# Loading K, Q and V for two groups at a time, and storing the last two groups over the SP queue, in a linear-attention kernel

## The chip, the cores and the metric

The kernel runs on one core of a Trainium2 chip. The metric is the device time of one execution in microseconds. The engines are TensorE (PE in the profile; PEld is its weight load), VectorE (DVE), ScalarE (ACT), GpSimd (POOL) and SyncE (SP). A DMA is issued by an engine (here GpSimd or SP) and carried out by the core's 16 DMA engines.

## What is computed

Batch 8, heads 12, sequence 512, head dimension 64, all float32:

```
Q_feat = np.maximum(0, Q) + 1
K_feat = np.maximum(0, K) + 1
KV = np.einsum('bhkd,bhkv->bhdv', K_feat, V)
K_sum = np.sum(K_feat, axis=2)
numerator = np.einsum('bhqd,bhdv->bhqv', Q_feat, KV)
denominator = np.einsum('bhqd,bhd->bhq', Q_feat, K_sum)
out = numerator / (denominator[:, :, :, None] + 1e-10)
```

There are 96 pairs of batch and head. Q, K, V and the output have 12.58 MB each, so 50.3 MB cross the memory interface once.

## The kernel before, in words

The 96 pairs are worked off in NG = 12 groups of eight. A group's slice of K, of Q, of V and of the output is 1 MiB in float32 each. K, Q and V are cast to bf16 by the DMA that loads them (512 KB in SBUF for each), all but the K of group 0, which SP loads as float32.

**Tiles.** `k_raw` and `q_raw` hold one group's K or Q; their pool has IN_BUFS = 4 buffers each. V goes into one of NV = 3 tiles `v_blk`, each with five blocks: blocks 0 to 3 hold V in a block-diagonal pattern (each block is filled by one DMA on its own 32 partitions and is zero elsewhere), and block 4 holds a pattern of ones that makes the K sums come out of the same matmul. The zeros and ones are written once, at the start, by DVE memsets (L206, L212, L224), ACT copies (L207, L213, L225) and small DVE copies (L210, L216, L228). Group g uses `v_blk[g % 3]`. Results go into `o_sb`, of which there are OUT_BUFS = 6.

**Functions.** `load_k` (L86) and `load_q` (L100) issue one DMA each, `load_v` (L93) four. `store` issues one DMA on GpSimd (L107), or, for the last group, two halves on SP (L110). `k_features` and `q_features` make max(x + 1, 1) on DVE, two instructions each (L116). `keys_values` does 32 matmuls (L141) into `kva_ps` and copies it into `kva_diag` on ACT (L151, L152). `transposes` turns the Q features on TensorE (L160) and copies them on ACT (L161). `output` does 32 matmuls (L173) into `o_ps` in four parts; DVE takes the reciprocal (L183) and multiplies (L184) part by part.

**Order.** The order on every engine is the order of the program text (`manual_schedule`); waits are put in by the framework where data or buffers need them. The loop at L231 does, for group g: features of g, transposes of g-1, output of g-2, keys_values of g, then the loads of group g+3 (AHEAD = 3) and the store of group g-3 (LAG = 3). So on GpSimd's queue the order is K, V, Q of group g+3 and then the store of g-3, and a waiting DMA holds up all that stand behind it. Before the loop the loads of groups 0, 1 and 2 are issued, between the memsets. After the loop the last group is finished and the stores of groups 8 to 11 are issued.

A tile may be written again when its readers are done: V of group g+3 waits for keys_values(g), K of group g+3 for k_features(g-1), Q of group g+3 for q_features(g-1).

Of the kernel before, what the change touches and what calls it, by code (L numbers as in the profile page):

```python
# [8 lines left out]
FP32 = mybir.dt.float32  # L9
BF16 = mybir.dt.bfloat16  # L10
ALU = mybir.AluOpType

BANK = 512
IN_BUFS = 4
OUT_BUFS = 6
LAG = 3
AHEAD = 3


@with_exitstack  # L20
def kernel(
# [4 lines left out]
    V: bass.AP,  # L26
    out: bass.AP,
):

# [5 lines left out]
    nc = tc.nc  # L37

    B, H, S, D = Q.shape
    P = 128  # L40
    C = 8
    C2 = 2 * C
    NPAIR = B * H * S // (P * C)
    NP = 4
    NG = NPAIR // NP
# [3 lines left out]
    def view(t, c):  # L49
        return t.flatten_outer_dims().rearrange("(n p c) d -> p n c d", p=P, c=c)  # L50

    q_dram = view(Q, C2)
    k_dram = view(K, C2)
    v_dram = view(V, C2)
    o_dram = view(out, C)

    const = ctx.enter_context(tc.tile_pool(name="const", bufs=1))
    head_pool = ctx.enter_context(tc.tile_pool(name="head_pool", bufs=1))
    in_pool = ctx.enter_context(tc.tile_pool(name="in_pool", bufs=IN_BUFS))
    feat_pool = ctx.enter_context(tc.tile_pool(name="feat", bufs=2))  # L60
# [6 lines left out]

    identity = const.tile([P, P], BF16, name="identity")
    NV = 3
    v_blk = [const.tile([P, 5, 2, C2, D], BF16, name=f"v_blk{i}") for i in range(NV)]  # L70
    ones = const.tile([P, 4], BF16, name="ones")
    zero = const.tile([P, 1], FP32, name="zero")
    kva_diag = [const.tile([P, 4, 2, D1], BF16, name=f"kva_diag{i}") for i in range(NV)]

    k_in = {}
    q_in = {}
    kfs = {}
# [1 line left out]
    qts = {}  # L79
    outs = {}  # L80

    def load_k(g):
        k_raw = (head_pool if g == 0 else in_pool).tile(
            [P, 2, C2, D], FP32 if g == 0 else BF16, name="k_raw"
        )
        (nc.sync if g == 0 else nc.gpsimd).dma_start(  # L86
            out=k_raw, in_=k_dram[:, g * 2 : g * 2 + 2]
        )
        k_in[g] = k_raw

    def load_v(g):
        for b in range(4):
            nc.gpsimd.dma_start(  # L93
                out=v_blk[g % NV][32 * b : 32 * b + 32, b],
                in_=v_dram[32 * b : 32 * b + 32, 2 * g : 2 * g + 2],
            )

    def load_q(g):
        q_raw = in_pool.tile([P, 2, C2, D], BF16, name="q_raw")
        nc.gpsimd.dma_start(out=q_raw, in_=q_dram[:, g * 2 : g * 2 + 2])  # L100
        q_in[g] = q_raw

    def store(g):
        o_sb = outs.pop(g)
        o_to = o_dram[:, g * NP : g * NP + NP]
        if g < NG - 1:
            nc.gpsimd.dma_start(out=o_to, in_=o_sb)  # L107
            return
        for h in range(2):
            nc.sync.dma_start(out=o_to[:, h:NP:2], in_=o_sb[:, h:NP:2])  # L110

    def edge(i):
        return v_blk[i][:, 4, :, :, 0:4].rearrange("p n c j -> p (n c) j")

    def feature(dst, src):
        nc.vector.tensor_scalar(  # L116
# [3 lines left out]
    def k_features(g):  # L120
        k_raw = k_in.pop(g)
        kf = feat_pool.tile([P, C2, 2, D], BF16, name="kf")
        for n in range(2):
            feature(kf[:, :, n], k_raw[:, n])
        kfs[g] = kf

    def q_features(g):
        q_raw = q_in.pop(g)
        qf = feat_pool.tile([P, C2, 2, D], BF16, name="qf")
        for half in range(2):  # L130
            cs = slice(half * C, half * C + C)
            feature(qf[:, cs].rearrange("p c n d -> p n c d"), q_raw[:, :, cs])
        qfs[g] = qf

    def keys_values(g):
        kf = kfs.pop(g)
        vb = v_blk[g % NV]
        kva_ps = psum_kva.tile([P, 5, D], FP32, name="kva_ps")
        for c in range(C2):
            for n in range(2):  # L140
                nc.tensor.matmul(  # L141
                    kva_ps[64 * n : 64 * n + 64],
                    lhsT=kf[:, c, n, :],
                    rhs=vb[:, :, n, c, :],
                    start=(c == 0),
                    stop=(c == C2 - 1),
                )
        kva = kva_diag[g % NV]
        for n in range(2):
            ps = slice(64 * n, 64 * n + 64)  # L150
            nc.scalar.copy(out=kva[ps, :, n, 0:D], in_=kva_ps[ps, 0:4, :])  # L151
            nc.scalar.copy(out=kva[ps, :, n, D], in_=kva_ps[ps, 4, 0:4])  # L152

    def transposes(g):
        qf = qfs.pop(g)
        qt = mid_pool.tile([P, C, P, 2], BF16, name="qt")
        for half in range(2):
            qt_ps = psum_qt.tile([P, C, P], BF16, name="qt_ps")
            for c in range(C):
                nc.tensor.transpose(qt_ps[:, c, :], qf[:, half * C + c, :, :], identity)  # L160
            nc.scalar.copy(out=qt[:, :, :, half], in_=qt_ps)  # L161
        qts[g] = qt

    def output(g):
# [26 lines left out]
                )  # L191
        outs[g] = o_sb

    with tc.manual_schedule():
        nc.gpsimd.memset(zero, 0.0)  # L195
        load_k(0)
        load_q(0)
        load_k(1)
        load_q(1)
        nc.vector.memset(ones, 0.0)  # L200
        for b in range(4):
            nc.vector.memset(ones[32 * b : 32 * b + 32, b : b + 1], 1.0)  # L202
        flat = [t.rearrange("p b n c d -> p (b n c d)").bitcast(FP32) for t in v_blk]
        width = flat[0].shape[1]
        part = width * 4 // 7
        nc.vector.memset(flat[0][:, 0:part], 0.0)  # L206
        nc.scalar.copy(  # L207
            out=flat[0][:, part:width], in_=zero.to_broadcast([P, width - part])
        )
        nc.vector.tensor_copy(out=edge(0), in_=ones[:, None, :].to_broadcast([P, 2 * C2, 4]))  # L210
        load_v(0)
        nc.vector.memset(flat[1][:, 0:part], 0.0)  # L212
        nc.scalar.copy(  # L213
            out=flat[1][:, part:width], in_=zero.to_broadcast([P, width - part])
        )
        nc.vector.tensor_copy(out=edge(1), in_=ones[:, None, :].to_broadcast([P, 2 * C2, 4]))  # L216
        make_identity(nc, identity)
        for t in kva_diag:
            nc.gpsimd.memset(t, 0.0)  # L219
        load_v(1)  # L220
        load_k(2)
        k_features(0)
        q_features(0)
        nc.vector.memset(flat[2][:, 0:part], 0.0)  # L224
        nc.scalar.copy(  # L225
            out=flat[2][:, part:width], in_=zero.to_broadcast([P, width - part])
        )
        nc.vector.tensor_copy(out=edge(2), in_=ones[:, None, :].to_broadcast([P, 2 * C2, 4]))  # L228
        load_v(2)
        load_q(2)  # L230
        for g in range(NG - 1):  # L231
            if g:
                k_features(g)
                q_features(g)
                transposes(g - 1)
            if g >= 2:
                output(g - 2)
            keys_values(g)
            if g + AHEAD < NG:
                load_k(g + AHEAD)  # L240
                load_v(g + AHEAD)
                load_q(g + AHEAD)
            if g >= LAG:
                store(g - LAG)
        last = NG - 1
        k_features(last)
        transposes(last - 1)
        output(last - 2)
        q_features(last)
        keys_values(last)  # L250
        transposes(last)
        output(last - 1)
        output(last)
        for g in range(last - LAG, NG):
            store(g)
# [30 lines left out]
```

## Time and profile before

| | us |
|---|---|
| median of 13 runs | 129.56 |
| lowest, highest | 129.02, 130.9 |
| the profiled execution's own time | 129.52 |
| its span, first to last instruction | 127.8 |

Busy shares of the span: TensorE 58%, weight load 42%, DVE 52%, ACT 37%, GpSimd 42%. The DMA traffic, by the profile's own count, is 37.75 MB read and 12.58 MB written, 394 GB/s over the span. The profile's row of GB/s counts the bytes that arrive, so a load that casts float32 to bf16 counts half of what it reads, and a store counts in full.

The page has the busy time of each engine, the span in 40 slices, the DMA queues, the chain of work that ended last, the costliest groups of instructions, and the DMA issues. Beside it the trace answers by time: the instructions of one engine in order, and busy time and DMA traffic in any stretch.

### The profile page before, as it was taken

How to read it: one execution, taken by the hardware profiler on the slowest of the kernel's cores; microseconds unless marked ns; L12 is line 12 of the kernel's file. 1: busy time of each engine (PE TensorE's matmuls, PEld its weight loads, DVE VectorE, ACT ScalarE, POOL GpSimd, SP SyncE). 2: the span in 40 equal slices, each digit the busy share in tenths (PEclk: the TensorE clock that was granted, in tenths of full speed). 3: DMA queues.
4: the chain of work that ended last, by engine and by line, in shares of the span. 5: the costliest groups of instructions: out<-in, count | busy, mean ns of one | idle time of the engine just before them, and what ended most of it. 6: DMA issues, size and time to landing. Idle time of an engine off the chain costs nothing.

```text
span 127.8 us, 2373 instructions
## 1 busy us (share of the span) xinstructions
PE 73.9 (58%) x960; PEld 54.0 (42%) x960; DVE 66.3 (52%) x155; ACT 47.2 (37%) x76; POOL 54.2 (42%) x92
## 2 busy tenths in 40 slices
PE   0000099839968297855804982991992896956000
PEld 0000077626656275644603651771661664834000
DVE  4898702085292955929309407615624825679300
ACT  7940006940546408291540063036027019180000
POOL 6695775516346274544442272282264240202000
PEclk9999999975699959999996577568559559996555
DMA  3999999999999999999999999999999999999970
GB/s 91 327 212 210 207 209 207 210 210 207 212 207 214 207 208 212 208 342 239 207 312 272 202 276 309 208 249 337 207 232 345 216 213 383 419 412 419 403 296 0
DMA packets 13914, 32.13 MB, mean 251 GB/s; under 512 B 1360, under 2 KB 1360, under 8 KB 13904
## 3 DMA queue, kind: packets, MB, share of 16 engines
q0 software_dynamic: 13088, 29.89, 99.4%
q1 hardware_dynamic: 816, 2.10, 4.6%
q8 instruction: 7, 0.11, 0.3%
q14 instruction: 3, 0.02, 0.0%
HBM read 37.75 MB, written 12.58 MB: 394 GB/s over the span
## 4 chain that ended last, share of the span: by engine, by line
DMA 63%; DVE 8%; PE 8%; POOL 8%; issue 6%; POOLq 0%
DMA k_raw<-in_K_dram 28%; DMA q_raw<-in_Q_dram 25%; DMA out_dram<-o_sb 10%; DVE o_sb L184 6%; POOL v_blk L93 6%; PE kva_ps L141 5%; PE qt_ps L160 2%; POOL q_raw L100 1%; PE o_ps L173 1%; DVE recip L183 1%; POOL k_raw L86 1%; DVE qf L116 1%; POOL zero L195 0%; POOLq L107 0%; POOLq L93 0%
## 5 line engine op out<-in xcount | busy, mean ns | idle before, releaser
L141 PE MATMUL kva_ps<-v_blk,kf 128*64 128x320 bf16 x384 | 42.3, 396 | 15.8 <-DMA v_blk<-in_V_dram 15.8
L141 PEld LDWEIGHTS <-kf 128*64 128x64 bf16 x384 | 28.8, 147 | 25.0 <-DVE qf L116 15.7
L93 POOL DMA_DIRECT2D v_blk<-in_V_dram x48 | 26.4, 554 | 28.0 <-DMA k_raw<-in_K_dram 12.1
L173 PE MATMUL o_ps<-kva_diag,qt 128*64 128x130 bf16 x384 | 21.1, 251 | 28.6 <-DVE o_sb L184 28.1
L184 DVE TENSOR_TENSOR o_sb<-o_ps,recip 128x512 f32<-128x512 f32 x48 | 33.2, 692 | 1.7
L151 ACT CAST kva_diag<-kva_ps 64x256 bf16<-64x256 f32 x24 | 8.9, 371 | 66.4 <-PE kva_ps L141 66.1
L161 ACT COPY qt<-qt_ps 128x1024 bf16<-128x1024 bf16 x24 | 29.6, 1301 | 0.3
L173 PEld LDWEIGHTS <-qt 128*64 128x64 bf16 x384 | 14.0, 123 | 34.6 <-DVE o_sb L184 32.8
L116 DVE TENSOR_SCALAR qf<-q_raw 128x1024 bf16<-128x1024 bf16 x24 | 9.2, 427 | 32.5 <-DMA q_raw<-in_Q_dram 32.5
L107 POOL DMA_DIRECT2D out_dram<-o_sb x11 | 8.5, 771 | 21.3 <-DMA q_raw<-in_Q_dram 7.0
L116 DVE TENSOR_SCALAR kf<-k_raw 128x1024 bf16<-128x1024 bf16 (+1 forms) x24 | 10.9, 498 | 11.1 <-DMA k_raw<-in_K_dram 5.6
L160 PE MATMUL qt_ps<-identity,qf 128*128 128x128 bf16 x192 | 14.0, 231 | 0.0
L160 PEld LDWEIGHTS <-qf 128*128 128x128 bf16 x192 | 11.9, 105 | 4.4 <-issue 4.2
L183 DVE RECIPROCAL recip<-o_ps 128x8 f32<-128x8 f32 x48 | 9.6, 199 | 4.9 <-PE o_ps L173 4.9
L86 POOL DMA_DIRECT2D k_raw<-in_K_dram x11 | 7.8, 713 | 8.7 <-DMA out_dram<-o_sb 5.5
L100 POOL DMA_DIRECT2D q_raw<-in_Q_dram x12 | 8.8, 730 | 4.2 <-DMA v_blk<-in_V_dram 2.5
L152 ACT CAST kva_diag<-kva_ps 64x4 bf16<-64x4 f32 x24 | 4.1, 169 | 0.0
L206 DVE MEMSET v_blk<- 128x2925 f32 x1 | 2.5, 2496 | 0.7 <-DVE ones L202 0.7
L224 DVE MEMSET v_blk<- 128x2925 f32 x1 | 2.5, 2496 | 0.6 <-issue 0.6
L212 DVE MEMSET v_blk<- 128x2925 f32 x1 | 2.5, 2496 | 0.6 <-issue 0.6
L219 POOL MEMSET kva_diag<- 128x520 bf16 x3 | 2.0, 718 | 0.0
L207 ACT COPY v_blk<-zero 128x2195 f32<-128x2195 f32 x1 | 2.0, 2019 | 0.0
(15 smaller groups left out, 7.9 us busy)
## 6 DMA issues: line engine op xcount, KB each, us to landing
out_dram<-o_sb POOLq DMA_DIRECT2D x11, 1024.0 KB, 11.9
q_raw<-in_Q_dram POOLq DMA_DIRECT2D x12, 512.0 KB, 10.8
v_blk<-in_V_dram POOLq DMA_DIRECT2D x48, 128.0 KB, 9.4
k_raw<-in_K_dram POOLq DMA_DIRECT2D x11, 512.0 KB, 12.0
k_raw<-in_K_dram SPq DMA_DIRECT2D x1, 1024.0 KB, 4.8
out_dram<-o_sb SPq DMA_DIRECT2D x2, 512.0 KB, 5.9
```

The lines of the kernel that those rows point to most:

```text
L86: (nc.sync if g == 0 else nc.gpsimd).dma_start(out=k_raw, in_=k_dram[:, g * 2 : g * 2 + 2])
L93: nc.gpsimd.dma_start(out=v_blk[g % NV][32 * b : 32 * b + 32, b], in_=v_dram[32 * b : 32 * b + 32, 2 * g : 2 * g + 2],)
L100: nc.gpsimd.dma_start(out=q_raw, in_=q_dram[:, g * 2 : g * 2 + 2])
L107: nc.gpsimd.dma_start(out=o_to, in_=o_sb)
L116: nc.vector.tensor_scalar(out=dst, in0=src, scalar1=1.0, scalar2=1.0, op0=ALU.add, op1=ALU.max)
L141: nc.tensor.matmul(kva_ps[64 * n : 64 * n + 64], lhsT=kf[:, c, n, :], rhs=vb[:, :, n, c, :], start=(c == 0), stop=(c == C2 - 1),)
L151: nc.scalar.copy(out=kva[ps, :, n, 0:D], in_=kva_ps[ps, 0:4, :])
L160: nc.tensor.transpose(qt_ps[:, c, :], qf[:, half * C + c, :, :], identity)
L161: nc.scalar.copy(out=qt[:, :, :, half], in_=qt_ps)
L173: nc.tensor.matmul(ops[c // 4][64 * j : 64 * j + 64, c // 2 % 2, (c % 2) * W : (c % 2) * W + W], lhsT=qt[:, c, 32 * b : 32 * b + 32, :], r ...
L183: nc.vector.reciprocal(out=recip, in_=cells[:, :, :, :, D:D1])
L184: nc.vector.tensor_tensor(out=o_sb[:, h:NP:2, 4 * i : 4 * i + 4].rearrange("p n (b c) d -> p b c n d", b=2), in0=cells[:, :, :, :, 0:D], i ...
```

## The change

K and Q are loaded for two groups with one DMA, and V for two groups with four DMAs, for groups 2 and 3, 4 and 5, 6 and 7, 8 and 9. Groups 0, 1, 10 and 11 are loaded one by one as before. The K and Q tiles are twice as large and there are two of each (IN_BUFS = 2), so the space is the same. The three V tiles become one tile `v_all` of nine blocks for two double buffers: blocks 0 to 3 are buffer 0, blocks 5 to 8 buffer 1, and block 4 (the ones) is shared; a matmul reads blocks 0 to 4 or blocks 4 to 8. Each block holds two groups, and a group's half is `own(g)`.

The loads in the loop are issued after keys_values of the odd groups 1, 3, 5 and 7, for the pair that starts three groups on, in the order K, V, Q; for groups 10 and 11, after group 7, as K, V, Q of 10 and then K, V, Q of 11. The store of g-3 stays at its place in the loop, behind them. The stores of groups 10 and 11, and not of 11 alone, go over SP in halves. The zeroing at the start is cut differently: three blocks by DVE and two by ACT for group 0 and for group 1, then two blocks each by DVE and ACT for the pair of groups 2 and 3.

```diff
-IN_BUFS = 4
+IN_BUFS = 2
 OUT_BUFS = 6
 LAG = 3
-AHEAD = 3
...
-    v_blk = [const.tile([P, 5, 2, C2, D], BF16, name=f"v_blk{i}") for i in range(NV)]
+    v_all = const.tile([P, 9, 4, C2, D], BF16, name="v_all")
+    v_blk = [v_all[:, 5 * i : 5 * i + 4] for i in range(2)]
...
+    def own(g):
+        return slice(g % 2 * 2, g % 2 * 2 + 2)
+
+    def load_k(s, groups):
+        if groups == (0,):
+            k_raw = head_pool.tile([P, 2, C2, D], FP32, name="k_first")
+            nc.sync.dma_start(out=k_raw, in_=k_dram[:, 0:2])
+            k_in[0] = k_raw
+            return
+        if s not in k_bufs:
+            k_bufs[s] = in_pool.tile([P, 4, C2, D], BF16, name="k_raw")
+        ms = slice(groups[0] % 2 * 2, groups[-1] % 2 * 2 + 2)
+        nc.gpsimd.dma_start(
+            out=k_bufs[s][:, ms], in_=k_dram[:, 2 * groups[0] : 2 * groups[-1] + 2]
+        )
+        for g in groups:
+            k_in[g] = k_bufs[s][:, own(g)]
+
+    def load_v(s, groups):
+        ms = slice(groups[0] % 2 * 2, groups[-1] % 2 * 2 + 2)
         for b in range(4):
             nc.gpsimd.dma_start(
-                out=v_blk[g % NV][32 * b : 32 * b + 32, b],
-                in_=v_dram[32 * b : 32 * b + 32, 2 * g : 2 * g + 2],
+                out=v_blk[s % 2][32 * b : 32 * b + 32, b, ms],
+                in_=v_dram[32 * b : 32 * b + 32, 2 * groups[0] : 2 * groups[-1] + 2],
             )
...
+    def load(s):
+        pair = (2 * s, 2 * s + 1)
+        for groups in ((pair,) if s < NG // 2 - 1 else ((pair[0],), (pair[1],))):
+            load_k(s, groups)
+            load_v(s, groups)
+            load_q(s, groups)
 
     def store(g):
         o_sb = outs.pop(g)
         o_to = o_dram[:, g * NP : g * NP + NP]
-        if g < NG - 1:
+        if g < NG - 2:
             nc.gpsimd.dma_start(out=o_to, in_=o_sb)
             return
...
     def keys_values(g):
         kf = kfs.pop(g)
-        vb = v_blk[g % NV]
+        sb = g // 2 % 2
+        vb = v_all[:, 4 * sb : 4 * sb + 5, own(g)]
...
-            nc.scalar.copy(out=kva[ps, :, n, 0:D], in_=kva_ps[ps, 0:4, :])
-            nc.scalar.copy(out=kva[ps, :, n, D], in_=kva_ps[ps, 4, 0:4])
+            nc.scalar.copy(out=kva[ps, :, n, 0:D], in_=kva_ps[ps, sb : sb + 4, :])
+            nc.scalar.copy(out=kva[ps, :, n, D], in_=kva_ps[ps, 4 - 4 * sb, 0:4])
...
+        clear((0, 5), own(0), 3)
+        mark(own(0))
+        load_v(0, (0,))
+        clear((0, 5), own(1), 3)
+        mark(own(1))
         make_identity(nc, identity)
         for t in kva_diag:
             nc.gpsimd.memset(t, 0.0)
-        load_v(1)
-        load_k(2)
+        load_v(0, (1,))
+        load_k(1, (2, 3))
         k_features(0)
         q_features(0)
...
+        clear((5, 9), slice(0, 4), 7)
+        load_v(1, (2, 3))
+        load_q(1, (2, 3))
         for g in range(NG - 1):
...
             keys_values(g)
-            if g + AHEAD < NG:
-                load_k(g + AHEAD)
-                load_v(g + AHEAD)
-                load_q(g + AHEAD)
+            if g % 2 and g // 2 + 2 < NG // 2:
+                load(g // 2 + 2)
             if g >= LAG:
                 store(g - LAG)
```

`clear(blocks, ms, parts)` zeroes blocks up to `parts` on DVE and the rest on ACT; `mark(ms)` writes the ones of block 4 on DVE; `load_q` is changed as `load_k` is.

More of the change, by code (lines that the diff above doesn't have):

```diff
@@ L73 @@
     kva_diag = [const.tile([P, 4, 2, D1], BF16, name=f"kva_diag{i}") for i in range(NV)]
+    k_bufs = {}
+    q_bufs = {}
     k_in = {}
@@ L80, with load_q @@
     outs = {}
-    def load_k(g):
-        k_raw = (head_pool if g == 0 else in_pool).tile(
-            [P, 2, C2, D], FP32 if g == 0 else BF16, name="k_raw"
-        )
[L86 to L91, printed above, removed]
+    def own(g):
[11 more added lines that the diff above has]
+            out=k_bufs[s][:, ms], in_=k_dram[:, 2 * groups[0] : 2 * groups[-1] + 2]
+        )
+        for g in groups:
+            k_in[g] = k_bufs[s][:, own(g)]
+    def load_v(s, groups):
+        ms = slice(groups[0] % 2 * 2, groups[-1] % 2 * 2 + 2)
         for b in range(4):
             nc.gpsimd.dma_start(
-                out=v_blk[g % NV][32 * b : 32 * b + 32, b],
-                in_=v_dram[32 * b : 32 * b + 32, 2 * g : 2 * g + 2],
-            )
[L98 to L101, printed above, removed]
+                out=v_blk[s % 2][32 * b : 32 * b + 32, b, ms],
+                in_=v_dram[32 * b : 32 * b + 32, 2 * groups[0] : 2 * groups[-1] + 2],
+            )
+    def load_q(s, groups):
+        if s not in q_bufs:
+            q_bufs[s] = in_pool.tile([P, 4, C2, D], BF16, name="q_raw")
+        ms = slice(groups[0] % 2 * 2, groups[-1] % 2 * 2 + 2)
+        nc.gpsimd.dma_start(
+            out=q_bufs[s][:, ms], in_=q_dram[:, 2 * groups[0] : 2 * groups[-1] + 2]
+        )
+        for g in groups:
+            q_in[g] = q_bufs[s][:, own(g)]
+    def load(s):
[4 more added lines that the diff above has]
+            load_q(s, groups)
     def store(g):
@@ L110, in store @@
             nc.sync.dma_start(out=o_to[:, h:NP:2], in_=o_sb[:, h:NP:2])
-    def edge(i):
-        return v_blk[i][:, 4, :, :, 0:4].rearrange("p n c j -> p (n c) j")
     def feature(dst, src):
@@ L192, in output, with clear, mark @@
         outs[g] = o_sb
+    def clear(blocks, ms, parts):
+        for eng, bs in zip((nc.vector, nc.scalar), (slice(blocks[0], parts), slice(parts, blocks[1]))):
+            t = v_all[:, bs, ms].rearrange("p b m c d -> p b (m c d)").bitcast(FP32)
+            if eng is nc.vector:
+                eng.memset(t, 0.0)
+            else:
+                eng.copy(out=t, in_=zero[:, :, None].to_broadcast([P, t.shape[1], t.shape[2]]))
+    def mark(ms):
+        e = v_all[:, 4, ms, :, 0:4].rearrange("p m c j -> p (m c) j")
+        nc.vector.tensor_copy(out=e, in_=ones[:, None, :].to_broadcast([P, e.shape[1], 4]))
     with tc.manual_schedule():
         nc.gpsimd.memset(zero, 0.0)
[L196 to L199, printed above, removed]
+        for g in range(2):
+            load_k(0, (g,))
+            load_q(0, (g,))
         nc.vector.memset(ones, 0.0)
@@ L202 @@
             nc.vector.memset(ones[32 * b : 32 * b + 32, b : b + 1], 1.0)
[L203 to L216, printed above, removed]
+        clear((0, 5), own(0), 3)
[3 more added lines that the diff above has]
+        mark(own(1))
         make_identity(nc, identity)
@@ L219 @@
             nc.gpsimd.memset(t, 0.0)
-        load_v(1)
-        load_k(2)
+        load_v(0, (1,))
+        load_k(1, (2, 3))
         k_features(0)
         q_features(0)
[L224 to L230, printed above, removed]
+        clear((5, 9), slice(0, 4), 7)
+        load_v(1, (2, 3))
+        load_q(1, (2, 3))
         for g in range(NG - 1):
```

## The prediction, made before the changed kernel ran

> **What bounds the kernel now.** I read the 40 slices first, then busy time and traffic by stretch, then DVE and GpSimd in order of time. The slices say that the DMA engines never rest:
>
> ```profile
> DMA  3999999999999999999999999999999999999970
> GB/s 91 327 212 210 207 209 207 210 210 207 212 207 214 207 208 212 208 342 239 207 312 272 202 276 309 208 249 337 207 232 345 216 213 383 419 412 419 403 296 0
> ```
>
> The rate row counts arriving bytes: 210 is 420 GB/s read by a casting load, as fast as the 419 of the stores at the end. By stretch (last two columns: DMA share, GB/s):
>
> ```profile
> 26.00:54.00 28.00, 20.87 (x286) 15.54 (x288) 18.39 (x48) 11.04 (x19) 13.32 (x22) 0.82 1.12 210
> ...
> 107.00:118.00 11.00, 7.48 (x128) 5.55 (x128) 8.97 (x23) 4.80 (x8) 1.50 (x2) 0.90 1.03 418
> 118.00:123.00 5.00, 0.29 (x6) 0.04 (x2) 1.24 (x3) 0.00 (x0) 0.00 (x0) 0.50 1.02 402
> ```
>
> Compute engines wait for loads; the DVE timeline shows Q of groups 3 to 10 landing, each releasing DVE (start, duration, ..., idle before):
>
> ```profile
> 34.23 0.76 DVE L116 TENSOR_SCALAR qf<-q_raw 128x1024 bf16<-128x1024 bf16 x2 [3.63 <-DMA q_raw<-in_Q_dram]
> 41.71 0.76 DVE L116 TENSOR_SCALAR qf<-q_raw 128x1024 bf16<-128x1024 bf16 x2 [2.66 <-DMA q_raw<-in_Q_dram]
> 49.26 0.76 DVE L116 TENSOR_SCALAR qf<-q_raw 128x1024 bf16<-128x1024 bf16 x2 [2.76 <-DMA q_raw<-in_Q_dram]
> 56.76 0.76 DVE L116 TENSOR_SCALAR qf<-q_raw 128x1024 bf16<-128x1024 bf16 x2 [2.70 <-DMA q_raw<-in_Q_dram]
> ...
> 97.56 0.76 DVE L116 TENSOR_SCALAR qf<-q_raw 128x1024 bf16<-128x1024 bf16 x2 [4.17 <-DMA q_raw<-in_Q_dram]
> ```
>
> From 34.23 to 56.76 three groups of loads pass, 22.53/3 = 7.51 us each, 2.5 per MiB. So the n-th MiB in queue order lands at about 4.2 + 2.5n: Q3, the 12th, at 34.2; Q4, the 15th, at 41.7. From 56.76 to 97.56 each group also has a store: 40.80/4 = 10.20, so a store there costs 2.69, against 1.049 MB / 418 GB/s = 2.51 among stores: 0.18 more. All 48 MiB with 5 such stores give 4.2 + 120 + 0.9 = 125.1. The last store, issued on SP at 119.30, takes 5.9 us: 125.2. The other 2.6 us of the 127.8 are the close of the program, and 1.72 lie around the span. So the time is the sum of DMA work, and compute matters only where it leaves the queue empty.
>
> GpSimd waits, too. V's first DMA of group 5 waits, as do the other three:
>
> ```profile
> 42.26 0.54 POOL L93 DMA_DIRECT2D v_blk<-in_V_dram  x1 [1.64 <-DMA q_raw<-in_Q_dram]
> 44.51 1.76 POOL L93 DMA_DIRECT2D v_blk<-in_V_dram  x3 [1.71 <-DMA k_raw<-in_K_dram]
> ```
>
> By the chain of waits the K that landed at 44.23 was issued at 32.29, eight GpSimd DMAs earlier. The same count holds at 29.47 (K issued at 17.93) and 70.13 (store issued at 57.31): at most eight are under way, some 4 to 5 MiB.
>
> **What the skill says.** "DMA: Bandwidth & Descriptors", section "Issuing engines are not separate DMA queues": queues of all engines share 16 DMA engines, so moving a store to SP saves issue time only. The trace agrees: SP's stores end at 402 GB/s, not above 418. Same page, "Anatomy of one DMA": a fixed cost of about 2 us per DMA, mostly completion latency. Here it hides behind queued work: K of group 5 landed 2.5 us after Q4 (44.23 - 41.71), and V (four DMAs) with Q took 49.26 - 44.23 = 5.03, again 2.5 each. "HBM Reference", "Specifications": a core alone streams about 425 GB/s; 418 to 420 here is near it.
>
> **The change, part by part.**
>
> *Fewer DMAs.* Before: 82 on GpSimd, 3 on SP. After: K 7, Q 8, V 2x4 + 4x4 + 2x4 = 32, stores 10 on GpSimd; 5 on SP. 85 become 62, 23 fewer. V's three extra DMAs cost at most 5.03 - 2x2.5, about 0.05 us, so one costs 0 to 0.02: a gain of 0 to 0.4. A cost below nothing has no reason, the bytes and pieces being the same. I take 0.2. GpSimd's issue time (0.54 for V, 0.72 for K, 0.78 for a store) falls by up to 16 x 0.54 + 8 x 0.72 + 0.78 = 15 us of its 54 (less what a larger DMA takes longer), off the path: GpSimd idles waiting for landings.
>
> *Stores in fewer islands.* Now stores 0 to 4 stand singly between loads. After, the loads of 6 and 7 come before stores 0 and 1, those of 8 and 9 before 2 and 3, and all other loads before 4: two islands. If the 0.18 belongs to changing direction, 3 x 0.18 = 0.54 is saved; if to each store, one store, 0.18. I take 0.54.
>
> *Store 10 on SP.* No bytes saved. If its 1.049 MB run at 402, as the last stretch does, and not 418, that is 0.10 lost; if SP's slowness is just the end's, 0. I take 0.10. On SP it stands ahead of store 11 and both wait for DVE alone; nothing else is queued on SP. Store 11 is no longer late: compute ends earlier (below).
>
> *Loads issued later or earlier.* At the start K0, Q0, K1, Q1, 4 MiB, keep the queue full to about 12.5. DVE's memset is 3072 elements instead of 2925 (2.50 us, so 2.62): V0 starts 0.1 later, hidden. The pair's clear is 4096 per engine, 3.5 us on DVE (2.5 now) and 3.7 on ACT: V of 2 and 3 goes out near 15, when V0 and V1 still have until about 17.5. Zero; without this cover it is 1 us.
>
> The tight place is the pair 6 and 7. K waits for k_features(3), V for keys_values(3), and behind both on GpSimd stand Q, store 0 and store 1. The pair's Q of 2 and 3 is again the 12th MiB, landing at 34.2. Then DVE: features 0.76, output(0) 4 x 0.84, features of 3 at 1.5: 40.0. TensorE: keys_values(2) from 37.0 (as keys_values(3) now), 2.34 at full and 4.48 at half clock, transposes 1.07, output(1) with two evacuations before its last matmuls, about 2.6; keys_values(3) from 43.0 to 45.2 and ending 45.4 to 50. The queue then holds K, V, Q of 4 and 5 and K of 6 and 7, to the 20th MiB: 2.5 x 20 + 2.5 = 52.5 (landing less some 1.7). V needs 0.54 to issue and 1 to 1.5 to run (the first DMAs are issued at 0.74 to 1.3 and reach 410 GB/s in the fourth microsecond). Margin 0.5 to 5 us: no gap, and I charge 0. If the cover is gone, each microsecond of lateness is one of time. For pair 8 and 9, stores 0 and 1 lengthen the queue: V leaves by 65, work until 72.5. The eight-DMA limit becomes looser in bytes, since K and Q now hold 2 MiB.
>
> *The end.* Q11 is now the 41st MiB, behind five stores; after, it is the 40th, behind four: it lands at 4.2 + 100 + 0.4 = 104.6, not 4.2 + 102.5 + 0.9 = 107.6. Compute, which ends at 119.27 now, ends near 116 (3 earlier, as its last data); six stores of GpSimd and two of SP keep the DMA engines full past it. Six output buffers make output(10) wait for store 4, the 41st MiB, near 107, just when it is wanted: 0 to 1 us inside that slack.
>
> **Sum,** against the profiled execution: 129.52 - 0.20 - 0.54 + 0.10 = 128.88, call it **128.9**. That execution lies 0.04 below the median, which I neglect.
>
> **Rivals.**
> *Deeper queue pays more (127.9).* From Q1's landing at 13.13 to Q3's at 34.21 eight MiB took 21.08, not 20.0, while GpSimd waited at the limit of eight. If larger DMAs regain that microsecond: 128.9 - 1.0. Against: the rate row shows no dip there.
> *Starved at the pair (131.1, slower).* keys_values(3) ends after about 51 and V of 6 and 7 goes out into an empty queue. It decides from half-clock matmuls (4.48, as keys_values(2) takes now) plus one wait that I lack, for instance if the one big `v_all` makes keys_values wait for a V load of the other buffer. Price: keys_values(3) at 53, plus 2 to start, less 52.5: about 2.2 us. Against: today's store of half an interleaved `o_sb` tile went out at 117.62, before the other half was written, so waits follow parts of tiles.
> *Nothing changes (129.5).* The 0.18 is per store or of another cause, the DMAs cost 0, SP gives back the rest.
>
> **Numbers.** The forecast has 0.56, its own range 128.4 to 129.5; the deeper queue 0.18; starvation 0.20; nothing 0.06. About 0.5%, 0.65 us, is what a measurement of this kernel can tell from no change, so the borders are 128.9 and 130.2: the forecast sits on the border and is halved (0.28 faster, 0.27 same, 0.01 slower). Faster 0.46, same 0.33, slower 0.21. The range, 127.8 to 131.2, takes in the centres of all cases.
>
> **What would show it.** Right: 210 arriving or 418 storing in every slice from 3 us to the end; Q of 2 and 3 landing near 34.2, Q of 8 and 9 near 84.6; DVE's last multiply near 116; end of traffic 0.6 earlier. Wrong: a slice under 180 near 52 (starvation), pure loads above 430, or stores on SP below 390 while GpSimd's queue also stores.

## The result, and the profile after

The changed kernel takes 135.39 us (median of 11 runs) against 129.59 (48 runs of the kernel before): a ratio of 1.0454, 95% interval 1.0424 to 1.0485. It is slower by 5.9 us, where 128.9 was forecast, with a range from 127.8 to 131.2. The profiled execution took 134.78 us with a span of 133.0, against 129.52 and 127.8.

The slices of the changed kernel's page, 3.3 us each, show the place at once: the DMA engines, which never rested before, stand empty in the sixth slice and run at half rate around it.

```profile
DMA  3999508899999999999999999999999999999994
GB/s 95 320 211 211 110 0 112 142 201 211 211 210 214 209 209 213 213 211 209 211 217 388 343 210 209 209 217 381 352 200 209 211 210 362 415 421 415 410 400 161
```

The same by stretch (the last two columns are DMA share and GB/s arriving):

```profile
15.00:20.00 5.00, 0.77 (x5) 0.34 (x7) 4.21 (x6) 0.00 (x0) 1.30 (x2) 1.00 0.02 4
20.00:27.00 7.00, 6.14 (x59) 4.37 (x57) 5.08 (x6) 2.68 (x6) 4.35 (x8) 1.00 0.85 131
27.00:69.00 42.00, 24.12 (x349) 18.05 (x345) 19.39 (x50) 14.04 (x26) 10.96 (x17) 0.80 1.12 210
```

Against the 210 of a full queue, 5 us at 4 GB/s and 7 us at 131 lose 5 x 206/210 + 7 x 79/210 = 7.5 us. From 27 us on the rate is as before.

Why the queue ran out is told by two engines. DVE, in order of time (start, duration, instruction, idle time before it and what ended it):

```profile
4.52 0.14 DVE L228 COPY v_all<-ones 128x128 bf16<-128x128 bf16 x1
15.79 2.62 DVE L222 MEMSET v_all<- 128x3072 f32 x1 [11.13 <-DMA v_all<-in_V_dram]
...
41.53 0.76 DVE L139 TENSOR_SCALAR qf<-q_raw 128x1024 bf16<-128x1024 bf16 x2 [9.28 <-DMA q_raw<-in_Q_dram]
```

and GpSimd:

```profile
4.90 2.12 POOL L107 DMA_DIRECT2D v_all<-in_V_dram  x4 [1.32 <-DVE v_all L228]
...
18.70 2.77 POOL L107 DMA_DIRECT2D v_all<-in_V_dram  x4 [9.69 <-DVE v_all L228]
21.47 0.77 POOL L98 DMA_DIRECT2D k_raw<-in_K_dram  x1
```

The second memset, which zeroes group 1's half of blocks 0 to 2, waits 11.1 us for V of group 0, which goes into the *other* half. The two touch no common byte. The chain of waits shows which load ended the wait (start, duration; DVEq is DVE's sequencer):

```profile
5.96 9.06 DMA v_all<-in_V_dram
15.03 0.03 issue
15.05 0.02 DVEq L222
```

It is the third of group 0's four V loads, into block 2, the last one that lies between the memset's first and last byte. The fourth, into block 3, landed at 15.7, and the wait had ended before. ACT's second clear, of blocks 3 and 4, waited for no load, but for the ones of group 0, which lie in the gap between its two stretches and which it doesn't touch either (x2: its third clear follows at once):

```profile
4.69 5.40 ACT L224 COPY v_all<-zero 128x2048 f32<-128x2048 f32 x2 [0.76 <-DVE v_all L228]
```

Behind the memset on DVE stand the ones of group 1, and on GpSimd the V loads of group 1 wait for those, and the K load of groups 2 and 3 stands behind them. When they go out at 18.70, what was queued before is long done (the rate falls at 15). Q of groups 2 and 3, the 12th MiB, lands at 41.5; the prediction had 34.2.

The 7.5 us are not all in the time. The end of the program gave some back; SP's waits after its last DMA show it, in the kernel before:

```profile
SPq L281 <- DMA out_dram<-o_sb: 5.0, 2, 3.8
SPq L281 <- PEq L281: 2.5, 2, 2.0
```

and in the changed kernel:

```profile
SPq L301 <- DMA out_dram<-o_sb: 6.2, 4, 2.6
...
SPq L301 <- PEq L301: 0.7, 2, 0.5
```

The longest of SP's last waits falls from 2.0 to 0.5 us. The profile puts it down to TensorE's sequencer (PEq), but TensorE's last matmul before was over at 118.3. The engine that comes late is GpSimd: its closing instruction, DRAIN, begins behind its last store and is the longest of three (ns min/median/max, first and last start), in the kernel before and in the changed kernel:

```profile
L281 POOLq DRAIN  x3: 51/108/10797, 116.2 to 127.5; - x3
...
L301 POOLq DRAIN  x3: 51/101/14414, 116.2 to 132.7; - x3
```

It ends at 127.0 before, 2.0 us after the last store on SP has landed (125.0), and at 130.6 in the changed kernel, 1.5 us ahead of that (132.1). I call the stretch from the end of traffic to the end of the span the close. Traffic ended at about 124.3 of 127.8 before (3.5 us left), and at about 131.3 of 133.0 after (1.7).

### The profile page after: what moved, and what is told of

Read it like the earlier page. It is cut to its first block, busy times and chain, and to the rows that moved or that the text cites. A ratio compares the mean times of both kernels' runs of the same rounds, so it can differ in the third digit from the quotient of the medians.

```text
span 133.0 us, 2337 instructions
## 1 busy us (share of the span) xinstructions
PE 68.1 (51%) x960; PEld 50.1 (38%) x960; DVE 65.4 (49%) x154; ACT 48.7 (37%) x76; POOL 39.7 (30%) x67
## 4 chain that ended last, share of the span: by engine, by line
DMA 55%; DVE 20%; PE 14%; issue 4%; POOL 2%; DVEq 0%; POOLq 0%
DMA q_raw<-in_Q_dram 41%; DMA v_all<-in_V_dram 14%; DVE o_sb L208 8%; PE kva_ps L165 8%; DVE v_all L222 7%; PE qt_ps L184 3%; PE o_ps L197 3%; DVE recip L207 2%; POOL v_all L107 2%; DVE qf L139 1%; DVE kf L139 1%; DVE ones L237 0%; DVE v_all L228 0%; DVE ones L235 0%; POOLq L116 0%
## 5 line engine op out<-in xcount | busy, mean ns | idle before, releaser
L165 PE MATMUL kva_ps<-v_all,kf 128*64 128x320 bf16 x384 | 38.4, 366 | 20.1 <-DVE kf L139 19.1
L197 PE MATMUL o_ps<-kva_diag,qt 128*64 128x130 bf16 x384 | 19.6, 238 | 35.8 <-DVE o_sb L208 35.2
L165 PEld LDWEIGHTS <-kf 128*64 128x64 bf16 x384 | 26.4, 136 | 28.4 <-DVE kf L139 19.6
L107 POOL DMA_DIRECT2D v_all<-in_V_dram x32 | 18.6, 586 | 37.3 <-PE kva_ps L165 13.4
L222 DVE MEMSET v_all<- 128x3072 f32 (+1 forms) x3 | 8.7, 2903 | 12.6 <-DMA v_all<-in_V_dram 11.1
L139 DVE TENSOR_SCALAR kf<-k_raw 128x1024 bf16<-128x1024 bf16 x22 | 8.2, 416 | 5.6 <-DMA k_raw<-in_K_dram 5.6
L98 POOL DMA_DIRECT2D k_raw<-in_K_dram x7 | 5.2, 742 | 19.2 <-DVE kf L139 10.1
L116 POOL DMA_DIRECT2D q_raw<-in_Q_dram x8 | 6.0, 752 | 6.5 <-DMA q_raw<-in_Q_dram 5.1
L224 ACT COPY v_all<-zero 128x2048 f32<-128x2048 f32 (+1 forms) x3 | 7.3, 2464 | 0.8 <-DVE v_all L228 0.8
L139 DVE TENSOR_SCALAR kf<-k_first 128x1024 bf16<-128x1024 f32 x2 | 1.3, 683 | 0.0
```

The costliest lines, as they stand in the source:

```text
L107: nc.gpsimd.dma_start(out=v_blk[s % 2][32 * b : 32 * b + 32, b, ms], in_=v_dram[32 * b : 32 * b + 32, 2 * groups[0] : 2 * groups[-1] + 2],)
L139: nc.vector.tensor_scalar(out=dst, in0=src, scalar1=1.0, scalar2=1.0, op0=ALU.add, op1=ALU.max)
L165: nc.tensor.matmul(kva_ps[64 * n : 64 * n + 64], lhsT=kf[:, c, n, :], rhs=vb[:, :, n, c, :], start=(c == 0), stop=(c == C2 - 1),)
L197: nc.tensor.matmul(ops[c // 4][64 * j : 64 * j + 64, c // 2 % 2, (c % 2) * W : (c % 2) * W + W], lhsT=qt[:, c, 32 * b : 32 * b + 32, :], r ...
L222: eng.memset(t, 0.0)
L224: eng.copy(out=t, in_=zero[:, :, None].to_broadcast([P, t.shape[1], t.shape[2]]))
```

## The experiments

Each ratio is to the kernel before, run beside it on the same chip.

**1. Clears by block.** Theory: a clear of several blocks in one instruction has gaps between its stretches, and the framework that puts in the waits took it as one range from its first byte to its last, so that it met the V loads in the gaps. Here each instruction covers one unbroken stretch.

```diff
-            t = v_all[:, bs, ms].rearrange("p b m c d -> p b (m c d)").bitcast(FP32)
-            if eng is nc.vector:
-                eng.memset(t, 0.0)
-            else:
-                eng.copy(out=t, in_=zero[:, :, None].to_broadcast([P, t.shape[1], t.shape[2]]))
+            for i in bs:
+                t = v_all[:, i, ms].rearrange("p m c d -> p (m c d)").bitcast(FP32)
+                if eng is nc.vector:
+                    eng.memset(t, 0.0)
+                else:
+                    eng.copy(out=t, in_=zero.to_broadcast([P, t.shape[1]]))
```

> The changed kernel with its clears cut into one instruction per block, so that each covers one unbroken stretch of a partition; the same bytes are zeroed. Theory (the second DVE clear was made to wait for V of group 0, because its three separated stretches are taken as one range that includes the rows in between): the 11.1 us wait of DVE at 4.7 us is gone, the DMA engines do not run empty between 15 and 21 us, Q of groups 2 and 3 lands near 34.2 instead of 41.5, and the time falls by about 7.3 us, to about 127.5 (0.985 of before). Rival (any two writes into the one V tile are ordered, whatever their place): the wait stays and the time stays near 135. Second rival (the pair loads themselves cost, later in the kernel): the wait goes, but the time stays above 130.

Measured: 127.83 us, 0.9869 (0.9840 to 0.9899). The slices of this kernel's page have no hole, and DVE goes from memset to memset:

```profile
DMA  3999999999999999999999999999999999999993
```

```profile
4.82 0.91 DVE L223 MEMSET v_all<- 128x1024 f32 x1
...
34.57 0.76 DVE L139 TENSOR_SCALAR qf<-q_raw 128x1024 bf16<-128x1024 bf16 x2 [10.01 <-DMA q_raw<-in_Q_dram]
```

Q of groups 2 and 3 lands at 34.6, and 7.6 us of the time are gone (1.0454 to 0.9869, times 129.6). ACT's wait for the ones is gone as well. Both rivals fall: writes into one tile are not ordered as such, and the pair loads are no cost.

**2. Clears as bf16.** Which property of the clear made its range inexact?

```diff
-            t = v_all[:, bs, ms].rearrange("p b m c d -> p b (m c d)").bitcast(FP32)
+            t = v_all[:, bs, ms].rearrange("p b m c d -> p b (m c d)")
```

> The changed kernel with its clears written as bf16, without the view as float32; each is still one instruction over separated stretches. If it is the float32 view that makes the place of the clear inexact, the wait goes here too and the time is that of the clears by block, about 127.5, plus nothing for the longer ACT clears. If it is the separated stretches in one instruction, the wait stays: about 135.

Measured: 128.05 us, 0.9886 (0.9854 to 0.9919). The wait is gone with the same stretches in one instruction, so it took both: several stretches in one instruction (experiment 1) and the view as float32. The trace of this kernel:

```profile
6.45 2.62 DVE L222 MEMSET v_all<- 128x3072 uint32 x1 [0.58 <-issue]
```

**3. Clears ahead of the load.** The third way out: no clear of that buffer follows a load into it.

```diff
         clear((0, 5), own(0), 3)
         mark(own(0))
-        load_v(0, (0,))
         clear((0, 5), own(1), 3)
         mark(own(1))
+        load_v(0, (0,))
```

> The changed kernel with the clear and the ones of group 1's half moved ahead of the load of V of group 0, so that no clear of that buffer follows a load into it. Theory: V of group 0 starts some 3 us later (near 7.7), which is hidden as the queue holds work to about 12.5; the wait is gone and the time is about 127.5, as with the clears by block. Rival (the pair loads cost): above 130.

Measured: 127.97 us, 0.9898 (0.9836 to 0.9960), as expected: the later start of V of group 0 is hidden.

**4. The wait alone, in the kernel before.** The opposite test: add the stall without the change.

```diff
+    seen = const.tile([P, 4], BF16, name="seen")[64:96]
...
         load_v(0)
+        nc.vector.tensor_copy(out=seen, in_=v_blk[0][64:96, 2, 0, 0, 0:4])
         nc.vector.memset(flat[1][:, 0:part], 0.0)
```

> The kernel before with one DVE copy of 4 elements put ahead of the second memset, that reads rows which the third V load of group 0 brings: the wait alone, without any other part of the change. Theory: DVE stands from about 5 to 15 us, V of group 1 goes out near 19, the DMA engines run empty between 15 and 21, and the time rises by about 7 us, to 136.5 (1.055). Rival (the stall costs because of the pairs, whose loads cannot fill up later): under 133.

Measured: 136.35 us, 1.0566 (1.0519 to 1.0614), 7.3 us. DVE in order of time:

```profile
15.07 0.16 DVE L213 COPY seen<-v_blk 32x4 bf16<-32x4 bf16 x1 [10.57 <-DMA v_blk<-in_V_dram]
15.89 2.50 DVE L214 MEMSET v_blk<- 128x2925 f32 x1 [0.66 <-issue]
```

The stall costs the old kernel as much as the new one. Pairs have no part in it.

**5. Store 10 on SP, in the kernel before.** With the stall out, the changed kernel is 1.3% faster than the kernel before. Which part does it?

```diff
-        if g < NG - 1:
+        if g < NG - 2:
```

> The kernel before with one edit: the store of group 10 goes over SP in halves too. My prediction's term: 0.1 us slower (129.7). Theory from the two traces: from the end of traffic to the end of the span were 3.5 us before and 1.7 in the changed kernel, and this comes from GpSimd's last store being over early; then about 1.5 us faster, 128.0 (0.988). Rival (the shorter close belongs to the other parts): 129.6.

Measured: 128.09 us, 0.9888 (0.9857 to 0.9919): 1.45 us faster from the moved store alone, where the prediction had 0.10 slower. Traffic ends at about 124.2, as before; the close is shorter:

```profile
SPq L281 <- DMA out_dram<-o_sb: 6.3, 4, 2.7
...
SPq L281 <- PEq L281: 0.7, 2, 0.5
...
L281 POOLq DRAIN  x3: 51/101/15662, 109.4 to 126.0; - x3
```

GpSimd's last store is now store 9, issued at 109.43, and its DRAIN ends at 125.1, ahead of the last landing on SP (125.4).

**6. Pairs without the moved store.** Clears by block, with the edit of experiment 5 undone (`NG - 1`).

> The changed kernel with clears by block, and the store of group 10 back on GpSimd (only group 11 on SP): the pair loads without the moved store. Theory (the pair loads bring nothing, all of the gain is the shorter close that the moved store brings): the end of traffic to the end of the span is 3 us or more again, and the time is 129.3 or more (0.998 to 1.003). Rival (the pair loads bring it): it stays near 127.8 (0.987).

Measured: 128.94 us, 0.9948 (0.9928 to 0.9969), between the two theories: the pair loads with fewer islands of stores bring 0.67 us (0.40 to 0.93), the moved store the rest.

**7. All stores on GpSimd, in the kernel before** (`g < NG` in the edit of experiment 5).

> The kernel before with the store of group 11 as one DMA on GpSimd too. Theory on the close (after the last GpSimd DMA has landed, GpSimd needs some 2 us more before the program can end): the end of traffic to the end of the span is again 3 us or more, and the time is as before or slower, 129.5 to 130.5. Rival (the close is shorter because both last stores are on one queue, whichever it is): it falls to about 128.

Measured: 127.92 us, 0.9914 (0.9885 to 0.9943). The theory of the close fails here: the last store, on GpSimd, is issued at 119.91 and landed 4.8 us later, GpSimd's DRAIN ends only 0.4 us after that, and the span ends at 125.8.

**8. All stores on GpSimd, with clears by block** (the same edit on experiment 1).

> The changed kernel with clears by block and all stores on GpSimd, SP having only its first load. As the kernel before with all stores on GpSimd has a short close and 127.9, this should have it too: 127.6 to 128.2. If the place of the last two stores on SP has a worth of its own in the pair version, it is 129 or more.

Measured: 130.00 us, 1.0048 (1.0026 to 1.0070), the opposite of experiment 7. The longest last wait of SP is back:

```profile
SPq L302 <- PEq L302: 2.7, 2, 2.2
```

The last store, issued at 117.21, took 7.8 us to land, at 125.0; the DRAIN ends 2.5 us after that, and the span at 128.2. So one queue for the last stores is no sure way to a short close.

**9. Store 11 in quarters on SP, in the kernel before.** Is it the number of SP's DMAs?

```diff
         for h in range(2):
-            nc.sync.dma_start(out=o_to[:, h:NP:2], in_=o_sb[:, h:NP:2])
+            for n in range(h, NP, 2):
+                nc.sync.dma_start(out=o_to[:, n : n + 1], in_=o_sb[:, n : n + 1])
```

> The kernel before with the store of group 11 on SP in quarters; store 10 stays on GpSimd. It tells what the short close hangs on. If it is that the last two stores are split between GpSimd and SP, the close stays 3 us or more: 129.5. If it is how many instructions or DMAs SP's program has (3 before and with the wait alone, 1, 5 or 9 in all kernels with a short close), it falls: near 128.0.

Measured: 129.35 us, 0.9978 (0.9962 to 0.9994); the longest last wait is 1.8 us, so the close stays long: the DRAIN ends at 126.8, 1.7 us after the last landing on SP. It isn't the number.

**10. Stores 8 to 11 on SP** (clears by block, `NG - 4`).

> The changed kernel with clears by block and the stores of groups 8 and 9 on SP in halves too. Theory on the close: GpSimd's last DMA is already over long before the end when only stores 10 and 11 are on SP, so nothing more is gained: 127.8, within 0.3 (0.985 to 0.989). Rival (each store moved to SP saves time): 1 us faster.

Measured: 128.58 us, 0.9950 (0.9932 to 0.9969). The close is short (0.5 us), but moving two more stores brings nothing and loses about 1 us to experiment 1. Compute ends at 120.1 instead of 117.0: one multiply on DVE waits 3.0 us for a store to free its buffer, which the theory had left out.

**11. Single loads in the order of the pairs.** Clears by block, every load of a pair issued as two.

```diff
+        if s < NG // 2 - 1:
+            for f in (load_k, load_v, load_q):
+                for g in pair:
+                    f(s, (g,))
+            return
...
```

> The changed kernel with clears by block, and every load of a pair issued as two loads of one group each, in the same order (K, K, V, V, Q, Q): 20 + 4 more DMAs on GpSimd and nothing else. My prediction's term: 23 fewer DMAs gain 0 to 0.4 us, so this should be 0 to 0.4 slower than clears by block (127.8 to 128.2, 0.987 to 0.990 of before). Rival (large DMAs matter, each has a fixed cost in the stream): 1 us slower or more.

Measured: 131.33 us, 1.0180 (1.0137 to 1.0223): some 4 us slower than pairs (1.0180 against 0.9869), well over the rival's 1 us. It is not spread over the DMAs, though. The rate holds near 210 to 61 us (208 from 40 on), and then has two holes, each about the landing of a pair's first Q (61.8 and 84.0), with its second Q next in the queue:

```profile
61.00:62.00 1.00, 0.82 (x21) 0.56 (x18) 0.14 (x1) 0.97 (x3) 0.00 (x0) 1.00 1.18 180
62.00:63.00 1.00, 0.00 (x0) 0.00 (x0) 0.97 (x4) 1.00 (x2) 0.61 (x1) 1.00 1.18 127
...
83.00:84.00 1.00, 0.00 (x0) 0.00 (x0) 0.01 (x1) 0.00 (x0) 0.00 (x0) 0.50 1.00 119
84.00:85.00 1.00, 0.00 (x0) 0.00 (x0) 0.96 (x4) 0.00 (x0) 0.61 (x1) 0.50 1.00 121
```

The queue is not short of work in them. Before the first hole GpSimd had issued, behind the second Q, two stores, two K and two V loads, 4.5 MiB, none of which had landed, and the DMA share (the last column but one) is 1.00 to 1.18:

```profile
56.88 1.55 POOL L138 DMA_DIRECT2D out_dram<-o_sb  x2
58.40 1.48 POOL L98 DMA_DIRECT2D k_raw<-in_K_dram  x2
59.82 1.12 POOL L107 DMA_DIRECT2D v_all<-in_V_dram  x2
```

**12. The same with the V loads in another order** (blocks 0, 2, 1, 3).

> The single loads in pair order (131.3 us), with the four V loads of a group issued in the order of blocks 0, 2, 1, 3 instead of 0, 1, 2, 3. If a V load of 32 partitions uses half of the DMA engines, and the two halves drift apart until the limit of eight stops one, this brings the halves closer and regains part: under 130.5. If the loss is of another kind, 131.3.

Measured: 131.18 us, 1.0098 (1.0070 to 1.0125). By the median nothing is regained; by the ratio, 130.9 us, a part is, less than was expected of the theory. The holes remain (the slice from 81 to 84 us has 157 GB/s). The run decides nothing: that two halves drift apart is not shown, and what makes the holes stays open.

## Why the prediction was wrong

**The step that failed** is "Loads issued later or earlier": "V of 2 and 3 goes out near 15, when V0 and V1 still have until about 17.5. Zero". It priced the longer clears and did not ask what the second clear waits for. That clear starts at 15.79 and not near 5, V of group 1 goes out at 18.70, and the queue is empty from 15. The cost is 7.3 (the stall alone) to 7.6 us (its removal). The cost of that step "without this cover" was given as 1 us; the cover, ten microseconds of queued loads, was gone entirely, since a wait for a *landing* is as long as the queue itself.

**The right rival with the wrong place.** The prediction named one big `v_all` as a source of false waits, and looked for them in keys_values. It set the rival aside because a store of half an interleaved `o_sb` went out before the other half was written. That evidence was true and not to the point: it was an access in the tile's own type. The matmuls of the changed kernel are tracked exactly as well (keys_values(0) runs at 19.11 while V of group 1, in the same blocks, is still on its way). The one kind of access that no trace of before showed was several stretches under a float32 view; before, each clear was one stretch. (By its own terms the rival's price was 53 + 2 - 52.5 = 2.5 us, not 2.2. That it was the one case with a slower kernel is luck: its wait and its place were others.)

**Fewer DMAs and fewer islands**: predicted 0.20 + 0.54 = 0.74, measured 0.67 (0.40 to 0.93, experiment 6). The sum holds; its two terms were not measured apart. Pair loads with two stores between Qs take 84.37 - 64.31 = 20.06 us in experiment 1; less 6 x 2.5 = 15 for loads, a store took 2.53, where single islands took 2.69. That would support the 0.54, but the six MiB of loads just before, without a store, took 64.31 - 49.64 = 14.67, and with that a store took 2.70. So the trace doesn't settle the term. Experiment 11 warns against counting DMAs: cutting the pairs in their new order costs about 4 us, while the same singles in the old order run at full rate. As 4.5 MiB stood in the queue, too few bytes under way do not explain its holes; what does stays open.

**Store 10 on SP**: predicted +0.10, measured -1.45 (experiment 5). I took what follows the last landing, 2.6 us in the prediction, as fixed. The Trainium skill, "DMA: Bandwidth & Descriptors", section "Issuing engines are not separate DMA queues", has DMAs of all engines run on the same 16 DMA engines, and the trace agrees: the traffic ends no earlier (124.2). What is saved is behind the traffic.

**The tight pair**: predicted K of 6 and 7 at 40.0 and V between 45.4 and 50. In experiment 1 they go out at 39.65 and 46.96, and the rate holds 205 to 221 from 49 to 55. Right: no gap.

**The end**: predicted compute near 116, 116.97 in experiment 1. Right. In the changed kernel itself it ends at 125.1, with the traffic still full behind it.

**What lies behind the last byte.** In every trace the span ends 0.7 to 1.4 us after the later of two things: the last landing on SP, and the end of GpSimd's DRAIN. In 13 of the 14 traces the DRAIN ends 2.3 to 3.4 us after GpSimd's own last store has landed. So the close is long where that store lands late (the kernel before and experiments 4, 6, 8 and 9), and short where the DRAIN is over before the last store on SP has landed (the changed kernel and experiments 1 to 3, 5 and 10 to 12). That is what the theory put on record with experiment 7 said, and why store 10 on SP is worth 1.45 us.

**What stays open.** What GpSimd does in these 2.3 to 3.4 us no trace shows, and experiment 7 is an exception to them (0.4 us). There the chain of waits has an entry of 4.45 us named "issue" on GpSimd just before the last store, which went out 2.2 us after DVE had ended (117.75 to 119.91); perhaps this is the same work, done earlier. That was not tried.

## The best version

Clears by block (127.83 us), store 10 on SP in the old kernel (128.09) and all stores on GpSimd in the old kernel (127.92) all beat both kernels, and their intervals overlap. The one-line edit of experiment 5 has nearly all of the gain of the whole change (1.45 of 1.7 us).

## What to carry to other kernels

When separate buffers become parts of one tile, list every write and read of that tile in program order and ask which can be taken to overlap, the start-up clears too; one false wait on a load's landing costs the depth of the queue, here 7.5 us. Evidence that one kind of access is tracked by its parts says nothing on another kind, above all not on a view in another type. In a kernel bound by DMA, price what lies behind the last byte as well, and ask which engine is the last to be done there: here it was worth more than 23 saved DMAs and fewer islands together (1.45 against 0.67 us).

## What the runs showed of the hardware beyond that

With little queued, the casting loads ran unevenly. In the changed kernel V of group 1 and K of groups 2 and 3 were under way alone from 21 to 25 us, at 197 GB/s arriving in the first of these microseconds and at 117 to 123 in the other three, where a full queue brings 210. So refilling an empty queue cost 2.6 of the 7.5 us after the first new load had gone out. The Trainium skill, "SBUF — State Buffer", section "Door 1: The DMA port swizzle", says that 32 partitions, as each V load has, reach 8 of 16 ports, good for about 218 GB/s; the 197 fits that, but it does not explain 117 to 123. What does is not shown. DVE's third memset runs in the same stretch (21.12 to 24.59); whether it has a part was not tried.
